# Rotary positions by row swaps inside SBUF in place of a permutation product

## Chip, cores and metric

The kernel runs on one core of a Trainium2 chip. The metric is the time of one launch on the device, in microseconds. All data are fp32 in HBM; the weights are read once per launch.

## What is computed

One inference step of a two-layer backbone on 128 context tokens and 128 latent tokens, side by side as 256 columns. Each layer is a SwiGLU feed-forward half step, a token mixer with three branches, and another feed-forward half step. The mixer has a state-space scan, a differential attention and a pooling branch. Only the attention matters here: its queries and keys of the latent tokens carry two-dimensional rotary positions before the scores. Cut from the reference (`n_freq` is 16, a head has 64 features, `half` is 32):

```python
def rotate(u, pos):
    ang = pos.astype(jnp.float32)[:, None] * inv_freq
    cos = jnp.cos(ang)[None, :, None, None, :].astype(u.dtype)
    sin = jnp.sin(ang)[None, :, None, None, :].astype(u.dtype)
    u1, u2 = u[..., :n_freq], u[..., n_freq:]
    return jnp.concatenate([u1 * cos - u2 * sin, u1 * sin + u2 * cos], axis=-1)

half = DIFF_HEAD_DIM // 2
return jnp.concatenate([rotate(t[..., :half], pos_row), rotate(t[..., half:], pos_col)], axis=-1)

# latent path of the mixer
q = axial_rope(q, rows)
k = axial_rope(k, rows)
k_all = jnp.concatenate([k_ctx, k], axis=1)
s = jnp.einsum('bqhcd,bkhcd->bhcqk', q_blk, k).astype(jnp.float32) * (d ** -0.5)
```

So feature f of a group of 32 has its partner 16 features away: out = t * cos + partner(t) * (plus or minus sin). Scores are sums over the 64 features of a half head, so the order of features inside it is free as long as q, k and the cached keys share it. The keys of the context are an output as well (`new_cache_k`).

## The kernel before

Activations lie feature by token: 128 features on the partitions, 256 tokens on the free axis (0 to 127 context, 128 to 255 latent). Weights come as 486 tiles of 128 x 1024 fp32 (512 KB) in one list, `plan()`. Each is loaded from HBM by SyncE into a `raw` tile (4 buffers), rounded by ScalarE into the high half `wh` (`emit_hi`), and VectorE makes the low half `wl` as raw minus `wh` (`emit_lo`). TensorE then takes three products per 128 x 128 piece (`mm3`, `nat`): wh with the high half of the activations, wh with their low half, wl with their high half. At the end of each tile's products `end()` runs the casts up to 5 tiles and the subtractions up to 4 tiles ahead of the tile in use. The tile `raw` comes free when the subtraction has read it, and the next load waits for that.

The order of instructions is written out at build time. `Pace` is a small cost model: it keeps a clock per engine, a time at which each piece of each tile is ready, and a latency per engine (2.2 us for a DMA). Side work is written as generators (`att_rope`, `att_scores`, `ssd`, `ada_rows` and others). A generator yields the engine that leads its next step and the tiles that the step needs; `advance()`, called after every second weight piece, lets a step go when the model says that its tiles are ready (`due()`; two generators of the list `gens` are looked at together, each up to 4 us ahead of PE's clock). On the chip each engine works through its own queue in that order and waits on semaphores that the framework sets.

In the mixer, the tiles of interest come in the order K (8 tiles, line 1129), V (8 tiles by `nat`, line 1142), z (8 tiles, line 1150), a gate, a branch, a gate, a branch. After the K tiles, `att_scores` and `att_rope` are added as generators (lines 1137 and 1138), and `vc` is loaded (line 1140). `att_rope` (line 1239) makes four rotations per layer, one after another, for the latent columns of q and of k, four heads at a time (a strided 128 x 512 view `t`): a product with the constant `perm` on TensorE into a PSUM tile of tag `s1` (two buffers, shared by all side work), then on VectorE a multiplication with `sin` into the SBUF tile `sw` (tag `t512`, two buffers), a multiplication of `t` with `cos` in place, and an addition. `att_scores` takes the context's scores first ((0, 0) and (0, 1) in `ATT`); those of the latent tokens wait for the entry in `roped` of their four heads. PSUM tiles of the projections have tag `pm` (three buffers). The row sums of the modulation (`ada_rows`) run on VectorE between all this.

Of the kernel before, what the change touches and what calls it, by code (L numbers as in the profile page):

```python
# [13 lines left out]
ALU = mybir.AluOpType  # L14
AX = mybir.AxisListType.X

P = 128
# [18 lines left out]
OFF_Q = 2592  # L36
OFF_K = 3616
OFF_V = 4640
# [57 lines left out]
CST = {}  # L96
_o = 0
for _n, _w in (("ident", 128), ("ones", 128), ("sel", 2), ("uf", 128), ("ub", 128), ("p0", 128), ("p1", 128), ("p2", 128),
               ("p3", 128), ("cos", 128), ("sin", 128), ("perm", 128), ("bm", 16), ("ind", 2)):
    CST[_n] = (_o, _o + _w)  # L100
    _o += _w
CST_W = _o
# [3 lines left out]
def constants():  # L106
    c = np.zeros((P, CST_W), np.float32)
    k = np.arange(P)[:, None]
    m = np.arange(P)[None, :]

    def put(name, a):
        c[:, CST[name][0]:CST[name][1]] = a

    put("ident", k == m)
    put("ones", 1.0)
    put("sel", k % 32 == m[:, :2])
    put("uf", k <= m)
    put("ub", k >= m)
    put("bm", np.where(k < 64, 1.0, -1.0) * (k % 16 == m[:, :16]))
    put("ind", k // 16 % 2 == m[:, :2])  # L120
    for g, w in enumerate(WINDOWS):
        lo = np.clip(m - w // 2, 0, P)
        hi = np.clip(m + w - w // 2, 0, P)
        cnt = (hi - lo).astype(np.float32)
        put(f"p{g}", ((k >= lo) & (k < hi)).astype(np.float32) / cnt - (k == m).astype(np.float32))
    inv = (THETA ** (-np.arange(16, dtype=np.float64) / 16)).astype(np.float32)
    perm = np.zeros((P, P), np.float32)
    for r in range(P):
        d = r % 64
        half, f = d // 32, d % 16  # L130
        pos = (np.arange(P) // GRID_W) if half == 0 else (np.arange(P) % GRID_W)
        ang = pos.astype(np.float32) * inv[f]
        c[r, CST["cos"][0]:CST["cos"][1]] = np.cos(ang.astype(np.float64))
        c[r, CST["sin"][0]:CST["sin"][1]] = np.sin(ang.astype(np.float64))
        if d % 32 < 16:
            perm[r + 16, r] = -1.0
        else:
            perm[r - 16, r] = 1.0
    put("perm", perm)
    return c  # L140


def head_order():
    return [4 * (2 * hf + half) + j for hf in range(2) for j in range(4) for half in range(2)]


def chan_order():
    return np.concatenate([np.arange(h * 64, h * 64 + 64) for h in head_order()])
# [84 lines left out]
def pack_weights(I, seq):  # L233
    out = np.zeros((len(seq), P, 1024), np.float32)
    co = chan_order()
    ho = head_order()
    xcols = np.concatenate([co, np.arange(1024, 1536)]) + OFF_XBC
    zcols = co + OFF_Z
    dcols = np.array([OFF_DT + d * 16 + h for d in range(2) for h in ho])

    def cols(w):
        return w.reshape(KD, P, P).transpose(1, 0, 2).reshape(P, 1024)

    fout = {}
    for i, s in enumerate(seq):
        t, l = s[0], s[1]
        if t == "fin":
            out[i] = cols(I["ffn_w_in"][l, s[2], :, s[3] * P:(s[3] + 1) * P])
        elif t == "fout":
            key = (l, s[2])  # L250
            if key not in fout:
                w = I["ffn_w_out"][l, s[2]].reshape(KF, P, KD, P)
                fout[key] = w.transpose(2, 0, 1, 3).reshape(KD * KF, P, P)
            out[i] = fout[key][s[3] * 8:(s[3] + 1) * 8].transpose(1, 0, 2).reshape(P, 1024)
        elif t == "xbc":
            out[i] = cols(I["w_in"][l][:, xcols[s[2] * P:(s[2] + 1) * P]])
        elif t == "dt":
            w = np.zeros((D, P), np.float32)
            w[:, :32] = I["w_in"][l][:, dcols]
            out[i] = cols(w)  # L260
        elif t == "win":
            out[i] = cols(I["w_in"][l][:, s[2]:s[2] + P])
        elif t == "z":
            out[i] = cols(I["w_in"][l][:, zcols[s[2] * P:(s[2] + 1) * P]])
        elif t == "nat":
            w = I["w_in"][l][s[3] * 2 * P:(s[3] + 1) * 2 * P, s[2]:s[2] + 512]
            out[i] = w.reshape(2, P, 512).transpose(1, 0, 2).reshape(P, 1024)
        elif t == "pool":
            w = I["pool_map"][l].reshape(4, 2, P, 2, P).transpose(0, 3, 1, 2, 4).reshape(16, P, P)
            out[i] = w[s[2] * 8:(s[2] + 1) * 8].transpose(1, 0, 2).reshape(P, 1024)  # L270
        elif t == "br":
            w = I["w_branch"][l, s[2]]
            if s[2] == 0:
                w = w[co]
            out[i] = cols(w[:, s[3] * P:(s[3] + 1) * P])
        elif t == "wout":
            out[i] = cols(I["w_out"][l][:, s[2] * P:(s[2] + 1) * P])
    return out
# [31 lines left out]
def pack_small(I):  # L310
    x = np.concatenate([I["x_prompt"][0], I["x_sample"][0]], 0)
    xT = np.ascontiguousarray(x.T.reshape(KD, P, NT).transpose(1, 0, 2))
    cc = np.stack([I["c_ctx"], I["c"][0]], 0)
    cT = np.ascontiguousarray(cc.T.reshape(KD, P, 2).transpose(1, 0, 2))
    ck = np.ascontiguousarray(I["cache_k"][0].transpose(0, 3, 2, 1))
    cv = np.ascontiguousarray(I["cache_v"][0].reshape(DEPTH, P, 1024))
    ho = head_order()
    st = I["state_ssm"][0]
    h0 = np.zeros((DEPTH, P, 2, 2, 4, 64), np.float32)
    for T in range(8):  # L320
        for half in range(2):
            h = ho[2 * T + half]
            h0[:, 64 * half:64 * half + 64, T // 4, :, T % 4] = st[:, :, h].transpose(0, 3, 1, 2)
    return xT, cT, ck, cv, h0.reshape(DEPTH, P, 1024)
# [99 lines left out]
def backbone(ctx: ExitStack, tc: tile.TileContext, seq, wst, wada, wa0, wrow, xT_d, cT_d, cB_d, ck_d, cv_d, h0_d, prm_d, cst_d,  # L424
             y_d, nk_d, nv_d, ns_d):
    nc = tc.nc
    pace = Pace()
    clk = pace.clk
    V, S, T_, G = (Paced(pace, n, e) for n, e in
                   (("dve", nc.vector), ("act", nc.scalar), ("pe", nc.tensor), ("pool", nc.gpsimd)))  # L430
# [10 lines left out]
    def v3(t, a):  # L441
        return t.rearrange("p (a b) -> p a b", a=a)

    def nm(s):
        uid[0] += 1
        return f"{s}{uid[0]}"
# [10 lines left out]
    def tmp(tag, shape, dt=F32, bufs=None):  # L457
        return tp.tile(shape, dt, tag=tag, name=nm(tag), **({"bufs": bufs} if bufs else {}))
# [12 lines left out]
    def grab(tag, t):  # L471
        free[tag].remove(min(free[tag], key=lambda n: pace.last.get(n, 0.0)))
        return t

    def drop(tag, t):
        free[tag].append(t.tensor.name)

    def ps1(n=512):
        return grab("s1", pp.tile([P, n], F32, tag="s1", bufs=2, name=nm("s1")))
# [16 lines left out]
    def C(name):  # L496
        return cst[:, CST[name][0]:CST[name][1]]
# [66 lines left out]
    def load(out, src):  # L564
        nc.sync.dma_start(out=out, in_=src)
        pace.op("dma", out.free_size() * P * 4 / 360e3, [out], [])

    def load_more(limit):
        while st["load"] < min(limit, st["cap"]):
            i = st["load"]  # L570
            raws[i] = pace.slot("raw", RAW_BUFS, wp.tile([P, 1024], F32, tag="raw", bufs=RAW_BUFS, name=nm("raw")))
            load(raws[i], wst[i])
            st["load"] += 1
# [88 lines left out]
    def ada_load(item):  # L662
        l, i, k = item
        raw = big()
        load(raw, wada[l, k, :, i])
        return raw
# [25 lines left out]
    def ada_rows(us, last):  # L692
        us = list(us)
        s = []
        for b in range(2):
            s.append(big())
            load(s[b], cB_d[:, b])
# [351 lines left out]
    def mixer(l):  # L1049
# [86 lines left out]
        oh, ol = [None, None], [None, None]  # L1136
        add(att_scores(l, q8, kl8, kc3, roped, ats))
        add(att_rope(q, kl, roped))
        vc = big()
        load(vc, cv_d[l])  # L1140
# [98 lines left out]
    def att_rope(q, kl, roped):  # L1239
        for i in range(2):  # L1240
            for t in (v3(q[i], 4)[:, :, P:], v3(kl[i], 4)[:, :, P:]):
                yield "pe", t, "s1"
                ps = ps1(512)
                T_.matmul(ps, lhsT=C("perm"), rhs=t, start=True, stop=True)
                yield "dve", ps
                sw = tmp("t512", [P, 512])
                V.tensor_tensor(out=v3(sw, 4), in0=v3(ps, 4), in1=C("sin").unsqueeze(1).to_broadcast([P, 4, P]), op=ALU.mult)
                drop("s1", ps)
                V.tensor_tensor(out=t, in0=t, in1=C("cos").unsqueeze(1).to_broadcast([P, 4, P]), op=ALU.mult)
                yield "dve", t, sw  # L1250
                V.tensor_tensor(out=t, in0=t, in1=v3(sw, 4), op=ALU.add)
            roped[i] = True
# [563 lines left out]
```

## Time and profile before

| | us |
|---|---|
| median of 3 runs | 1560.96 (1560.48 to 1561.48) |
| the profiled execution | 1561.46 |
| its span, first to last instruction | 1559.70 |
| TensorE busy in it | 1529.8 |
| VectorE busy in it | 1320.7 |
| ScalarE busy in it | 853.8 |

The profile is one execution. Engines are PE (TensorE's matmuls), PEld (its weight loads), DVE (VectorE), ACT (ScalarE), POOL (GpSimd) and SP (SyncE, which issues the DMAs). A matmul's record reaches past the time at which the next one can begin, so the cost of one matmul in a row of them is read from start to start. Rows name a tile written, an arrow, and the tiles read, without buffer numbers; nearly all instructions have line 393 or 565, the helpers that record them, so they are told apart by tile. In the rows below, `s<-big,cst` with 512 columns is the product with `perm`, `t<-s,cst` is the multiplication with `sin`, `big<-big,cst` that with `cos`, and `big<-big,t` the addition. The first four rotations run at 427 to 442 us, the second four at 1179 to 1193 us.

### The profile page before, as it was taken

The page shows a single profiled execution, that of the slowest core. Times are in us where ns is not written, and L with a number is a line of the kernel's source. Part 1 is how long each engine was busy: PE and PEld are TensorE (multiplying, and loading weights), DVE is VectorE, ACT ScalarE, POOL GpSimd, SP SyncE. Part 2 cuts the span into 40 slices and gives each one's busy share as a digit, 9 for nine tenths or more (in the row PEclk, how much of TensorE's full clock was granted, in tenths as well). Part 3 has the DMA queues.
Part 4 walks back from the last instruction along what each step waited for, and adds up shares of the span by engine and source line. Part 5 has one row for each costly group of instructions (what it writes and reads, how often), then busy time and mean ns, then how long its engine had stood idle before and what let it go on. Part 6 is the DMA issues. An engine that isn't in the chain of part 4 may idle for free.

```text
span 1559.7 us, 30787 instructions
## 1 busy us (share of the span) xinstructions
PE 1529.8 (98%) x12062; PEld 1435.4 (92%) x12062; DVE 1320.7 (85%) x2412; ACT 853.8 (55%) x1538; POOL 59.0 (4%) x65
## 2 busy tenths in 40 slices
PE   6999999999999999999999999999999999999997
PEld 4988889999989999999899998998998999999986
DVE  5787698987888998999989999898879899888754
ACT  3564447654667446644447444575555754565442
POOL 0000002000001000100001000100000010010000
PEclk9999999999999999999999999999999999999998
DMA  9688775553664666688765877555466457568652
GB/s 371 215 331 297 264 266 165 186 188 123 237 221 159 230 227 231 217 313 286 254 224 190 297 272 268 178 189 175 143 221 232 162 198 262 175 203 281 217 179 82
DMA packets 98738, 348.26 MB, mean 223 GB/s; under 512 B 10913, under 2 KB 14625, under 8 KB 98465
## 3 DMA queue, kind: packets, MB, share of 16 engines
q1 hardware_dynamic: 98592, 346.30, 64.0%
q8 instruction: 95, 1.56, 0.4%
q14 instruction: 51, 0.41, 0.1%
HBM read 342.06 MB, written 4.19 MB: 222 GB/s over the span
## 4 chain that ended last, share of the span: by engine, by line
PE 78%; issue 12%; DVE 6%; DMA 2%; ACT 1%; POOL 1%; DVEq 0%; POOLq 0%; SPq 0%
PE pm L393 70%; PE s L393 6%; DVE big L393 2%; DVE wl L393 2%; PE pa L393 2%; DVE t1k L393 1%; DMA big<-wada 1%; POOL osr L393 1%; ACT big L393 1%; ACT wh L393 0%; DVE wide L393 0%; DMA x<-xT 0%; DVE sqa L393 0%; ACT L393 0%; DVE x L393 0%
## 5 line engine op out<-in xcount | busy, mean ns | idle before, releaser
L393 PE MATMUL pm<-big,wh 128*128 128x256 f32 (+2 forms) x6568 | 1293.3, 294 | 3.7 <-DVE big L393 2.2
L393 PEld LDWEIGHTS pm<-big,wh 128*128 128x128 f32 x6568 | 1030.0, 189 | 52.7 <-issue 19.7
L393 PE MATMUL pm<-big,wl 128*128 128x256 f32 (+1 forms) x3592 | 1005.1, 281 | 0.0
L393 PEld LDWEIGHTS pm<-big,wl 128*128 128x128 f32 x3592 | 676.8, 188 | 2.2
L393 DVE TENSOR_TENSOR wl<-raw,wh 128x1024 fp32r<-128x1024 f32 x481 | 587.5, 1227 | 9.5 <-ACT wh L393 8.9
L393 ACT CAST wh<-raw 128x1024 fp32r<-128x1024 f32 x481 | 502.0, 1049 | 138.5 <-PE pm L393 101.6
L393 DVE SCALAR_TENSOR_TENSOR big<-big,big 128x1024 f32<-128x1024 f32 x198 | 242.0, 1222 | 12.9 <-DMA big<-wrow 11.6
L393 ACT CAST big<-t1k 128x256 fp32r<-128x256 f32 x88 | 36.0, 409 | 156.5 <-DVE t1k L393 156.5
L393 ACT ACTIVATE big<-x,amod 128x128 fp32r<-128x128 f32 x96 | 33.6, 398 | 101.5 <-DVE x L393 82.6
L393 PE MATMUL pm<-wh,big 128*128 128x512 f32 x256 | 88.5, 409 | 0.0
L393 DVE TENSOR_TENSOR wide<-pm,rb 128x258 f32<-128x258 f32 (+1 forms) x108 | 45.2, 423 | 37.4 <-PE pm L393 30.8
L393 DVE SCALAR_TENSOR_TENSOR x<-pm,mods,x 128x128 f32<-128x128 f32 x152 | 43.7, 346 | 34.3 <-PE pm L393 34.1
L393 ACT COPY big<-pm 128x256 f32<-128x256 f32 (+2 forms) x88 | 31.2, 374 | 74.6 <-PE pm L393 73.8
L393 PEld LDWEIGHTS pm<-wh,big 128*128 128x128 f32 x256 | 48.1, 188 | 13.0 <-issue 2.1
L393 DVE TENSOR_TENSOR big<-t1k,big 128x256 fp32r<-128x256 f32 x128 | 55.8, 440 | 1.6 <-ACT big L393 0.9
L393 ACT ACTIVATE t1k<-wide 128x128 f32<-128x128 f32 (+1 forms) x96 | 33.6, 398 | 38.5 <-DVE wide L393 38.4
L393 PE MATMUL s<-big,big 128*64 128x128 f32 (+5 forms) x544 | 53.3, 303 | 0.0
L393 PE MATMUL pm<-wl,big 128*128 128x512 f32 x128 | 50.3, 393 | 0.0
L393 PEld LDWEIGHTS s<-big,big 128*64 128x64 f32 (+2 forms) x544 | 42.3, 164 | 5.3 <-issue 2.8
L393 ACT ACTIVATE t1k<-pm 128x256 f32<-128x256 f32 x58 | 22.3, 385 | 43.1 <-PE pm L393 43.1
L393 DVE TENSOR_TENSOR big<-big,big 128x256 f32<-128x256 f32 (+1 forms) x64 | 39.9, 623 | 3.3 <-ACT big L393 1.9
L393 DVE SCALAR_TENSOR_TENSOR big<-big,cw,big 128x252 f32<-128x252 f32 (+1 forms) x96 | 39.4, 487 | 2.8 <-ACT big L393 2.7
(146 smaller groups left out, 940.2 us busy)
## 6 DMA issues: line engine op xcount, KB each, us to landing
raw<-wst SPq DMA_DIRECT2D x486, 512.0 KB, 3.7
big<-wrow SPq DMA_DIRECT2D x96, 512.0 KB, 5.0
big<-wada SPq DMA_DIRECT2D x32, 512.0 KB, 5.6
big<-wa SPq DMA_DIRECT2D x16, 512.0 KB, 10.1
big<-cB SPq DMA_DIRECT2D x12, 512.0 KB, 7.7
x<-xT SPq DMA_DIRECT2D x1, 1024.0 KB, 4.9
big<-h SPq DMA_DIRECT2D x2, 512.0 KB, 4.4
ns<-t SPq DMA_DIRECT2D x8, 128.0 KB, 4.9
```

The lines of the kernel that those rows point to most:

```text
L393: r = fn(*a, **k)
```

## The change

The features of q, k and the cached keys are laid out in another order, made on the host in the weights' columns and in the cache: inside each 64 features the partner of a row stands 32 rows away. The constant `perm` goes. In `att_rope` the swapped copy of `t` is made by four transfers from SBUF to SBUF, each of 32 rows x 4 heads x 128 columns (64 KB, in runs of 512 bytes), issued by ScalarE on its own DMA queue (`swap`). The sign is in the constant `sin`. The step that leads a rotation is now one of `act` without a PSUM tile, and the `sin` multiplication reads `sw` in place. In the model each transfer takes 0.3 us on the DMA clock. The written keys `nk` go out in the new order, and the host sorts them back. Number and size of all other instructions stay as they are.

```diff
-               ("p3", 128), ("cos", 128), ("sin", 128), ("perm", 128), ("bm", 16), ("ind", 2)):
+               ("p3", 128), ("cos", 128), ("sin", 128), ("bm", 16), ("ind", 2)):
...
+def pair_order():
+    r = np.arange(P)
+    return r // 64 * 64 + r // 16 % 2 * 32 + r // 32 % 2 * 16 + r % 16
...
-            out[i] = cols(I["w_in"][l][:, s[2]:s[2] + P])
+            w = I["w_in"][l][:, s[2]:s[2] + P]
+            out[i] = cols(w[:, pair_order()] if OFF_Q <= s[2] < OFF_V else w)
...
-    ck = np.ascontiguousarray(I["cache_k"][0].transpose(0, 3, 2, 1))
+    ck = np.ascontiguousarray(I["cache_k"][0].transpose(0, 3, 2, 1)[:, pair_order()])
...
+    def swap(out, src):
+        nc.scalar.dma_start(out=out, in_=src)
+        pace.op("dma", 0.3, [out], [src])
...
             for t in (v3(q[i], 4)[:, :, P:], v3(kl[i], 4)[:, :, P:]):
-                yield "pe", t, "s1"
-                ps = ps1(512)
-                T_.matmul(ps, lhsT=C("perm"), rhs=t, start=True, stop=True)
-                yield "dve", ps
+                yield "act", t
                 sw = tmp("t512", [P, 512])
-                V.tensor_tensor(out=v3(sw, 4), in0=v3(ps, 4), in1=C("sin").unsqueeze(1).to_broadcast([P, 4, P]), op=ALU.mult)
-                drop("s1", ps)
+                for p in range(0, P, 32):
+                    swap(v3(sw, 4)[p:p + 32], t[p ^ 32:(p ^ 32) + 32])
+                yield "dve", sw
+                V.tensor_tensor(out=v3(sw, 4), in0=v3(sw, 4), in1=C("sin").unsqueeze(1).to_broadcast([P, 4, P]), op=ALU.mult)
                 V.tensor_tensor(out=t, in0=t, in1=C("cos").unsqueeze(1).to_broadcast([P, 4, P]), op=ALU.mult)
                 yield "dve", t, sw
                 V.tensor_tensor(out=t, in0=t, in1=v3(sw, 4), op=ALU.add)
...
-    nk = np.asarray(r["nk"]).transpose(0, 3, 2, 1)[None]
+    nk = np.asarray(r["nk"])[:, np.argsort(pair_order())].transpose(0, 3, 2, 1)[None]
```

## Rows read from the trace of the kernel before

**Rows 1.** The page, part 1: busy us, share of the span, instructions.

```profile
PE 1529.8 (98%) x12062; PEld 1435.4 (92%) x12062; DVE 1320.7 (85%) x2412; ACT 853.8 (55%) x1538; POOL 59.0 (4%) x65
```

**Rows 2.** The page, part 4: the chain that ended last, by engine.

```profile
PE 78%; issue 12%; DVE 6%; DMA 2%; ACT 1%; POOL 1%; DVEq 0%; POOLq 0%; SPq 0%
```

**Rows 3.** Windows: stretch; length; busy of PE, PEld, DVE, ACT, POOL; clock; DMA.

```profile
425.00:430.00 5.00, 5.00 (x37) 3.77 (x36) 5.00 (x6) 1.38 (x3) 0.00 (x0) 1.00 0.86 302
430.00:435.00 5.00, 5.00 (x20) 3.43 (x19) 5.00 (x10) 4.11 (x18) 0.00 (x0) 1.00 0.88 288
435.00:440.00 5.00, 5.00 (x24) 3.49 (x24) 5.00 (x8) 2.74 (x4) 0.00 (x0) 1.00 0.63 211
...
450.00:455.00 5.00, 5.00 (x25) 3.61 (x24) 4.18 (x8) 1.62 (x2) 0.00 (x0) 1.00 0.86 288
455.00:460.00 5.00, 5.00 (x39) 4.66 (x37) 2.98 (x9) 4.46 (x13) 0.00 (x0) 1.00 0.79 205
...
470.00:480.00 10.00, 10.00 (x86) 9.49 (x84) 9.82 (x23) 7.58 (x19) 0.00 (x0) 1.00 0.31 108
```

**Rows 4.** PE: all products with `perm` (min/median/max ns); timeline (start us, us) around one.

```profile
L393 PE MATMUL s<-big,cst x16: 590/592/697, 427.8 to 1187.3; 128*128 128x512 f32 x16
...
428.99 0.39 PE L393 MATMUL pm<-wl,big 128*128 128x512 f32 x1
...
429.68 0.39 PE L393 MATMUL pm<-wl,big 128*128 128x512 f32 x1
...
435.33 1.02 PE L393 MATMUL s<-big,cst 128*128 128x512 f32 x2
435.79 0.80 PE L393 MATMUL pm<-wh,big 128*128 128x512 f32 x1
436.42 0.40 PE L393 MATMUL pm<-wl,big 128*128 128x512 f32 x1
```

**Rows 5.** Groups of DVE instructions: busy us, mean ns, idle before.

```profile
L393 DVE TENSOR_TENSOR t<-s,cst 128x512 f32<-128x512 f32 x8 | 5.5, 688 | 0.0
L393 DVE TENSOR_TENSOR big<-big,cst 128x512 f32<-128x512 f32 x8 | 5.5, 688 | 0.0
```

**Rows 6.** Windows of `wl` on DVE; of `wh` on ACT; ACT timeline; ACT groups, 453 to 479.

```profile
0.00:425.90 425.90, 144.16 (x119) 1.00 0.68 240
0.00:443.20 443.20, 149.27 (x123) 1.00 0.68 241
0.00:478.90 478.90, 161.43 (x133) 1.00 0.67 236
...
0.00:425.90 425.90, 124.95 (x120) 1.00 0.68 240
...
426.11 0.43 ACT L393 COPY big<-pm 128x128 f32<-128x128 f32 x2 [1.44 <-PE pm L393]
...
L393 ACT ACTIVATE t1k<-pm 128x256 f32<-128x256 f32 x6 | 2.3, 391 | 4.2 <-PE pm L393 4.2
```

**Rows 7.** Page part 6 (KB, median us to landing); issues of `ns`, of `ck` (ns).

```profile
ns<-t SPq DMA_DIRECT2D x8, 128.0 KB, 4.9
...
nk<-big SPq DMA_DIRECT2D x2, 512.0 KB, 7.1
...
cT<-cT SPq DMA_DIRECT2D x1, 8.0 KB, 1.8
...
L1172 SPq DMA_DIRECT2D ns<-t x8: 423/424/1105, 342.6 to 1141.1; - x8
...
L565 SPq DMA_DIRECT2D big<-ck x2: 384/440/497, 402.4 to 402.8; - x2
...
DMA to landing us min/median/max: 4.9/5.6/6.3
```

**Rows 8.** PE timeline: the scores of latent queries, first and second four heads.

```profile
450.58 1.14 PE L393 MATMUL s<-big,big 64*128 64x256 f32 x8
...
468.08 1.13 PE L393 MATMUL s<-big,big 64*128 64x256 f32 x8
```

More of the change, by code (lines that the diff above doesn't have):

```diff
@@ L126, in constants @@
     inv = (THETA ** (-np.arange(16, dtype=np.float64) / 16)).astype(np.float32)
-    perm = np.zeros((P, P), np.float32)
     for r in range(P):
-        d = r % 64
+        d = pair_order()[r] % 64
         half, f = d // 32, d % 16
         pos = (np.arange(P) // GRID_W) if half == 0 else (np.arange(P) % GRID_W)
[L132 to L139, printed above, removed]
-    return c
+        ang = (pos.astype(np.float32) * inv[f]).astype(np.float64)
+        c[r, CST["cos"][0]:CST["cos"][1]] = np.cos(ang)
+        c[r, CST["sin"][0]:CST["sin"][1]] = np.sin(ang) if d % 32 >= 16 else -np.sin(ang)
+    return c
+def pair_order():
+    r = np.arange(P)
+    return r // 64 * 64 + r // 16 % 2 * 32 + r // 32 % 2 * 16 + r % 16
 def head_order():
```

## The prediction

> **What bounds the kernel now.** First the busy times of the engines [rows 1]: PE works 98% of the span, DVE 85%. Then the chain of work that ended last [rows 2]: PE holds 78% of it, so the end is mostly a sum of PE work. An average over the span doesn't say what the rotation costs, so next the stretch where it runs in layer 0, in windows [rows 3]. The reader is to see three things there. PE is busy 5.00 of every 5.00 us, at the full clock, 2.4 GHz. DVE is busy 5.00 of 5.00 as well from 425 to 440, has holes at 450 to 460 (4.18 and 2.98 of 5.00), and is nearly full again at 470 to 480. ACT has 1.38, 4.11 and 2.74 of 5.00. So what leaves PE here shortens the program, as long as DVE, which makes the low half of every weight tile, isn't made later than its lead allows. The lead is read from counts [rows 6], below.
>
> **What the change takes away.** Per layer four products with `perm`, eight in all; each is two records of one fp32 matmul, so sixteen [rows 4]. The duration of a record (590 ns) overlaps its neighbours, so I take start to start. The matmuls of the V projection stand 0.23 us apart: three of them from 428.99 to 429.68. The single product begins at 435.33, and the second matmul after it at 436.42; without 0.23 for the first one, the product holds PE for 436.42 - 0.23 - 435.33 = 0.86 us. Eight of these are 8 x 0.86 = 6.9 us of a PE that has no idle time beside them. The first product of a layer shows about 0.1 more, just behind the scores; I leave that out, since the scores hand over to the next product anyway. The two PSUM tiles of tag `s1` are also held less; nothing waits for them in this stretch, so that is worth nothing.
>
> **What it adds on DVE.** The multiplication with `sin` reads the swapped copy from SBUF instead of PSUM. Nearest rows [rows 5]: from PSUM 688 ns, and the multiplication with `cos`, of the same size and all in SBUF, 688 ns. Difference nothing. What is new is its wait: it now needs four transfers to have landed, and on DVE's queue stand behind it the subtractions `wl`, on which PE lives, the row sums of the modulation, and the softmax steps.
>
> **What it adds on ACT.** 16 issues per layer on ACT's queue, 32 in all. The trace has no DMA issued by ACT. The nearest rows are SP's [rows 7]: 0.42 us for `ns`, 0.38 at best and 0.50 for `ck`, so from 16 x 0.38 to 16 x 0.50, or 6.1 to 8.0 us per layer; below that, almost nothing, if ACT's engine works on what is queued while its sequencer issues. I take 0.42, that is 1.7 us per group of four and 6.7 us per layer. Behind these issues ACT holds the casts `wh`, the copies out of PSUM and the exponentials. ACT had (5.00 - 1.38) + (5.00 - 4.11) + (5.00 - 2.74) = 6.8 us free in the first three windows of [rows 3], and at 425.90 it had made 120 casts where DVE had made 119 subtractions [rows 6]: its casts are as far ahead of PE. A late copy out of PSUM is met by a third `pm` tile. So: nothing on PE; were that cover gone, up to 1.7 us a group, 13.6 us in all.
>
> **When the swapped copy lands.** Each transfer is 64 KB in runs of 512 bytes. Bounds from [rows 7]: 1.8 us for 8 KB, 7.1 for the 512 KB of `nk`, one of which goes out in this very stretch; `ns`, 128 KB, takes 4.9. I take about 4, a little below `ns`, since that writes to memory and the swap doesn't. With three issues before the last one that is 3 x 0.42 + 4 = 5.3 us from the first issue to the landing of all four. The planner gives the DVE step free only when its model says so: 4 x 0.3 + 2.2 = 3.4 us, counted from its DMA clock, on which the loads in front stand too (512 KB are 1.46 us there; `vc` is loaded just before the first rotation). So it hands the step to DVE after 3.4 to about 6 us, and meanwhile gives DVE other work. Real less planned: between 1.26 + 1.8 - 6 = -3 (no wait at all) and 1.26 + 7.1 - 3.4 = +5. I take 1 us of DVE standing still per rotation, four per layer.
>
> Here a rule speaks against the change. In the trace two `ck` loads issued 0.4 us apart, each in 512-byte runs, landed 4.9 and 6.3 us after issue [rows 7]: their latencies lie on top of each other. The Trainium skill, "DMA: Bandwidth & Descriptors", section "Rules for kernel authors", says to coalesce many small transfers, since under 64 KB one pays mostly overhead; and by the fixed 2.0 us of its section "Anatomy of one DMA" four transfers one after another would be over 8 us (an estimate from that page). By that each rotation would leave DVE about 2 to 5 us short; by the row it isn't so, because the four are in flight together.
>
> **What covers those 4 us.** The lead of the low halves [rows 6]. At 425.90 PE begins the first V tile, number 122 of the list (the copy of the last K tile follows at 426.11); DVE has begun 119 + 5 = 124 low halves, the five being those of the start. So two finished tiles lie ahead of the one in work, with the third in making, about 8 us at 2.8 us a tile (12 products of 0.23). At 443.20 it is the same: 128 begun, and PE, after four V tiles, at the 126th. At 478.90 it is thinner: 138 begun, the 138th just done, while PE works on the seventh z tile, the 136th (six z tiles have been copied out by 479); some 5 us. DVE makes up for lost time in the holes of 450 to 460, before that point. A PE that is 3.5 us earlier per layer takes as much from the lead: 5 - 3.5 = 1.5 us are left. So the cover holds in the sum, but not by much; I book 0.5 us for all places together where it doesn't.
>
> **The chain of rotations gets longer** and that is covered. A rotation took about 3 us of the chain (products at 427.8, twice at 430.8, at 435.3), and now takes 6 to 7, so the second ends near 440 and the fourth near 455. Their readers, the scores over latent keys, begin at 450.58 for the first four heads and at 468.08 for the others [rows 8].
>
> **Sum.** Profiled execution: 1561.46 (span 1559.70 and 1.76 around it). Less 6.9, plus 0.5: 1555.1. That execution stands 0.5 above the median of the runs, so 1560.96 - 6.4 = **1554.6 us**. A second queue in use might lengthen the start or the end; the trace shows only that all around the span is 1.76 us, so that is 0 to 1.8, and I take 0.
>
> **The rivals.**
> 1. DVE waits for the transfers and PE for DVE: slower. The mechanism is DVE's first-in-first-out queue at the `sin` multiplication. The four waits of a layer fall within some 25 us; cover is the 8 us of lead and 2.8 us of holes between 450 and 460, so from 2.7 us a rotation on PE begins to lose, and from 2.7 + 3.45 / 4 = 3.6 us it loses all that it won. At the upper bound of 5 us PE loses 20 - 10.8 = 9.2 us per layer, and the time is 1561 - 6.9 + 18.4 = 1572.5; at 4.5 it is 1568.5. For it: DVE full from 425 to 440, and `nk`, `cv` and weight loads in flight there. Against: the planner already waits, and fills the wait.
> 2. DVE is the real bound of the stretch, and PE's gain comes back as waits for low halves between 460 and 520: about 1561, between 1558 and 1564. For it: DVE at 9.82 of 10 at 470 to 480, and a lead of 5 us there. Against: 2 of 5 us free just before.
> 3. ACT's issues hold back copies out of PSUM: with two of eight groups badly placed, 2 x 1.7 = 3.4 us come back, 1558. Against: the third `pm` tile, and ACT's free time.
> 4. It doesn't take the product's time away, because PE would have stood still there: 1561. Against it are 5.00 of 5.00 us; no chance of its own.
> 5. PE gains more than the products, from the `s1` tiles or the 0.1 behind the scores: 1551 to 1552.
>
> **How the numbers follow.** My forecast (1552.5 to 1557) 0.56; rival 1, 0.12; rival 2, 0.18; rival 3, 0.11; rival 5, 0.03. About 0.2%, 3.1 us, is what a measurement of this kernel can tell from no change. Faster by more than that, below 1557.8: 0.56 + 0.03 + 0.09 of rival 3 = 0.68. Within it: 0.18 + 0.02 = 0.20. Slower, above 1564.1: 0.12. The range for 8 in 10 takes in the forecast, rival 3 and most of rival 2: 1552.0 to 1563.0.
>
> **What would show it.** The records with `cst` of 512 columns gone from PE and PE still busy 5.00 of 5.00 in the same windows: step right. DVE idle before `t<-t,cst`, released by a DMA, over 2.7 us each and then PE idle for `wl`: rival 1. PE idle for `wl` with no such wait: rival 2. ACT issues at 0.4 us and PE idle for `pm`: rival 3. Landings of the swaps at 3 to 5 us; at 7 my term for them is wrong. If the planner's new order moves a stall elsewhere, by more than 2 us, the sum is wrong for a reason that no step of it holds.

## The result, and the profile after

| | us |
|---|---|
| before, median of 4 runs beside it | 1561.22 (1560.48 to 1562.17) |
| changed, median of 4 runs | 1572.39 (1570.56 to 1575.12) |
| ratio, 95% interval | 1.0071 (1.0057 to 1.0084) |
| profiled execution after, its span | 1573.09, 1571.3 |

The change makes the kernel 11.2 us slower; 1554.6 was predicted, and 1563.0 was the upper end. First, PE in part 1 of the page after (busy us, share, instructions), against [rows 1]:

```profile
PE 1527.0 (97%) x12046; PEld 1435.2 (91%) x12046; DVE 1319.9 (84%) x2412; ACT 854.0 (54%) x1540; POOL 60.4 (4%) x65
```

Sixteen matmul records fewer, and PE is busy 2.8 us less, but the span is 11.6 longer: PE now stands still. The waits of PE (us in total, times, longest) name where; the lines shown are those that the kernel before does not have in this size:

```profile
PE pm L393 <- DVE x L393: 10.2, 1, 10.2
...
PE s L393 <- ACT big L393: 3.0, 2, 1.9
...
PE pm L393 <- DVE wide L393: 2.1, 4, 1.4
...
PE pm L393 <- ACT big L393: 1.0, 1, 1.0
```

The large one is a single hole, and it isn't at the rotations. It stands at the output projection of layer 1, some 140 us behind the last of them. Windows of the changed kernel (columns as in [rows 3]), and then its timeline there, first SP, then ACT, DVE and PE (start us, us, engine, line, operation, and in brackets the wait before it):

```profile
1330.00:1340.00 10.00, 10.00 (x87) 10.00 (x86) 7.52 (x14) 4.61 (x6) 0.00 (x0) 1.00 0.52 169
1340.00:1350.00 10.00, 2.49 (x21) 2.28 (x20) 3.90 (x7) 2.11 (x2) 0.00 (x0) 0.72 0.57 198
1350.00:1360.00 10.00, 7.04 (x38) 6.78 (x39) 9.25 (x23) 5.98 (x13) 0.00 (x0) 0.60 0.45 136
```

```profile
1337.37 0.90 SPq L565 DMA_DIRECT2D big<-cB  x2
1338.31 0.95 SPq L565 DMA_DIRECT2D big<-wrow  x2
...
1343.35 1.06 ACT L393 ACTIVATE big<-big 128x1024 f32<-128x1024 f32 x1 [5.77 <-DMA big<-cB]
...
1345.93 1.23 DVE L393 SCALAR_TENSOR_TENSOR big<-big,big 128x1024 f32<-128x1024 f32 x1 [7.87 <-DMA big<-wrow]
...
1351.93 0.60 DVE L393 SCALAR_TENSOR_TENSOR x<-pm,mods,x 128x128 f32<-128x128 f32 x2
...
1352.68 0.77 PE L393 MATMUL pm<-big,wh 128*128 128x256 f32 x2 [10.20 <-DVE x L393]
```

Read upward: PE waits for an addition to `x`; that waits for `mods`; `mods` waits for four multiplications of two row sums on DVE (1.22 us each, `big<-big,big` of 128x1024); these wait for two loads of `wrow`; and in front of them ACT has waited for two loads of `cB`. Loads of `cB` belong to a batch of row sums: page part 6 has 12 of them before and 14 after (KB, median us to landing). The code explains the extra batch:

```profile
big<-cB SPq DMA_DIRECT2D x12, 512.0 KB, 7.7
big<-cB SPq DMA_DIRECT2D x14, 512.0 KB, 7.3
```

```
if not row_todo or st["cur"] >= last - HOLD:      # in ada_rows: batch ends, HOLD = 5 tiles before `last`
    us.clear()
...
def need(*ms):                                    # called by gated_add at the first output tile
    late = [i for i, it in enumerate(row_todo) if it[:2] in ms]
    if late:
        side["slow"].append(Side(ada_rows([0] * (late[-1] + 1), 1 << 30)))
    settle(lambda: all(m in ada_done for m in ms))
```

The output projection of layer 1 needs 88 row sums, two instructions each. A batch gets its places from DVE's free time in the model and ends five tiles before its stage. Counted in the trace up to the first addition to `x` in that projection, DVE has run 182 such instructions before (88 row sums and 6 others) and 178 after: two row sums are missing, and `need` makes them there, with everything standing still. The two counts (us in total, mean ns, idle time before), before and after:

```profile
L393 DVE SCALAR_TENSOR_TENSOR big<-big,big 128x1024 f32<-128x1024 f32 x182 | 222.4, 1222 | 11.2 <-DMA big<-wrow 10.0 <-ACT big L393 0.4
L393 DVE SCALAR_TENSOR_TENSOR big<-big,big 128x1024 f32<-128x1024 f32 x178 | 216.8, 1218 | 12.2 <-DMA big<-wrow 10.2 <-ACT big L393 1.2
```

Up to 480 us, behind the rotations of layer 0, SP has issued 19 loads of `wrow` before and 18 after; up to 620 us it is 29 and 28, and up to 800 us 51 and 49. So the changed kernel falls one behind at the rotations and two behind by 800 us. (The runs e1 and e2 below are one behind at 480 us too, and have caught up by 620.)

In the hole PE's clock falls: PE stands still from 1342.5, and the granted clock is 0.50, that is 1.2 GHz, from 1346 to 1357 and 1.00, 2.4 GHz, from 1359 on (the windows above, 0.72 and 0.60, hold both levels). Groups of three products that start 0.36 us apart at 1358.4 start 0.64 apart at 1357.3. Together: the first product with the low half of the tile `wout` 2 of layer 1 starts 2.4 us earlier than before (1339.7 against 1342.1), that of `wout` 4 10.8 later (1358.6 against 1347.8), so the hole costs 13.2 us, of which 10.2 + 0.3 are standing still and most of the rest the lower clock.

What the change itself added looks as follows. Instructions by tile (ns min/median/max, first and last start), page part 6 (KB, us to landing), and the range of the landings:

```profile
L569 ACTq DMA_DIRECT2D t<-big x32: 592/612/1523, 427.2 to 1199.6; - x32
L393 DVE TENSOR_TENSOR t<-t,cst x8: 679/681/687, 438.8 to 1205.3; 128x512 f32<-128x512 f32 x8
...
DMA to landing us min/median/max: 2.0/4.5/7.2
```

```profile
t<-big ACTq DMA_DIRECT2D x32, 64.0 KB, 4.4
```

In the view of the tiles `t`, none of what DVE sat idle for is a DMA. The 3.0 us of `PE s <- ACT big` are the second scores of each layer, which must wait until ACT has read the first ones (here the first layer):

```profile
427.67 1.16 PE L393 MATMUL s<-big,big 64*128 64x128 f32 x16
436.48 1.16 PE L393 MATMUL s<-big,big 64*128 64x128 f32 x16 [1.16 <-ACT big L393]
```

They stand 8.8 us behind the first; before it was 13.1, with no wait:

```profile
426.70 1.16 PE L393 MATMUL s<-big,big 64*128 64x128 f32 x16
...
439.77 1.16 PE L393 MATMUL s<-big,big 64*128 64x128 f32 x16
```

In layer 1 the wait is 1.86. The 1.0 us of `PE pm <- ACT big` follows there: a product of the V projection needs a `pm` tile that ACT is to copy out, and the copy stands in ACT's queue behind the second exponentials, which begin at 1189.67:

```profile
1192.43 1.11 ACT L393 COPY big<-pm 128x512 f32<-128x512 f32 x2
1193.10 0.50 PE L393 MATMUL pm<-wh,big 128*128 128x512 f32 x1 [0.98 <-ACT big L393]
```

The line `DVE wide`, 1.4 us at the longest, stands at the second FFN of layer 1; the experiments come back to it.

### The profile page after: what moved, and what is told of

The parts are those of the page before. It is cut to its first block, busy times and chain, and to the rows that moved or that the text cites. A ratio compares the mean times of both kernels' runs of the same rounds, so it can differ in the third digit from the quotient of the medians.

```text
span 1571.3 us, 30803 instructions
## 1 busy us (share of the span) xinstructions
PE 1527.0 (97%) x12046; PEld 1435.2 (91%) x12046; DVE 1319.9 (84%) x2412; ACT 854.0 (54%) x1540; POOL 60.4 (4%) x65
## 4 chain that ended last, share of the span: by engine, by line
PE 76%; issue 12%; DVE 7%; DMA 3%; ACT 2%; POOL 0%; SPq 0%; DVEq 0%; POOLq 0%; ACTq 0%
PE pm L393 68%; PE s L393 6%; DVE big L393 2%; DVE wl L393 2%; PE pa L393 2%; DVE t1k L393 1%; DMA big<-wrow 1%; ACT big L393 1%; ACT wh L393 1%; DMA big<-cB 0%; DVE wide L393 0%; DMA big<-wada 0%; DMA x<-xT 0%; DMA raw<-wst 0%; DVE sqa L393 0%
## 5 line engine op out<-in xcount | busy, mean ns | idle before, releaser
L393 PE MATMUL pm<-big,wh 128*128 128x256 f32 (+2 forms) x6568 | 1295.8, 294 | 14.8 <-DVE x L393 10.2
L393 POOL TENSOR_TENSOR rsr<-rsv,halfc 128x2 f32<-128x2 f32 x9 | 6.3, 698 | 923.3 <-DVE rsv L393 923.3
```

Of the source, the lines that this page charges most:

```text
L393: r = fn(*a, **k)
```

## Experiments

All times are medians; each run has its own runs of the kernel before beside it (1561.3 to 1561.6), and the ratio to those decides. A profile is one execution, and executions differ by 1 to 2 us in their first 50 us alone, so only waits and local distances are compared between profiles. In the expectations, "row sum" at the first addition to `x` counts single instructions: two of them are one row.

| run | kernel | us | ratio (95%) |
|---|---|---|---|
| e1_hold4 | changed, HOLD 4 | 1559.44 | 0.9987 (0.9977 to 0.9998) |
| e2_noswap | changed, no exchange at all | 1557.54 | 0.9974 (0.9965 to 0.9984) |
| e3_before_late_rows | before, two row sums left over | 1574.64 | 1.0088 (1.0074 to 1.0101) |
| e4_act_cost | changed, ACT's issues in the model | 1560.64 | 0.9995 (0.9986 to 1.0004) |
| e5_rows_sooner | changed, ROW_LAG 1.0 | 1565.61 | 1.0025 (1.0016 to 1.0034) |
| e6_noswap_rows_sooner | no exchange, ROW_LAG 1.0 | 1555.71 | 0.9969 (0.9958 to 0.9980) |
| e7_before_rows_sooner | before, ROW_LAG 1.0 | 1560.68 | 1.0006 (0.9996 to 1.0016) |
| e8_sync_queue | e5 with transfers on SP's queue | 1566.00 | 1.0028 (1.0017 to 1.0040) |
| e9_cast_gate | e1 and a limit on casts | 1556.73 | 0.9969 (0.9957 to 0.9982) |
| e10_rows_sooner_cast_gate | e5 and the limit | 1559.90 | 0.9988 (0.9979 to 0.9998) |
| e11_cast_gate_exps_first | e9 and the limit at V | 1560.06 | 0.9986 (0.9978 to 0.9995) |
| **e12_table_load_told** | e9 and the table load in the model | **1553.95** | **0.9952 (0.9934 to 0.9970)** |
| e13_before_same_mends | before, with e12's three edits | 1560.76 | 1.0004 (0.9995 to 1.0013) |
| e14_noswap_same_mends | e12 with no exchange | 1555.33 | 0.9965 (0.9953 to 0.9977) |

### Is it the left-over row sums?

```diff
-HOLD = 5
+HOLD = 4
```


> The changed kernel with HOLD = 4 in place of 5, so that the row sums of a mixer may be begun one weight tile later; the plan then has all 16 row sums in the mixer of layer 0 and none left over at the first output tile of layer 1. Theory A (the loss is the two left-over row sums, made while PE stands still: the first use of output tile 4 of layer 1 lies 13.2 us later against before than that of output tile 2): 1572.4 - 13.2 = 1559, 1557 to 1561. Theory B (the loss is DVE's wait for the transfers, as in rival 1 of the prediction): HOLD does not touch that, 1571 to 1573.

```diff
-CAP = {..., ("mix", 1): (16,), ...}
+CAP = {..., ("mix", 1): (14,), ...}
```
(in the kernel before)


> The kernel before, products and all, with the number of row sums allowed in the mixer of layer 1 cut from 16 to 14, so that two are left over and made at the first output tile, as in the changed kernel. Theory A: 1561.2 + 13.2 = 1574, 1572 to 1576. Theory B: the two left-over sums are hidden or cheap, 1561 to 1564.

HOLD 4 gives the missing rows their places, the trace has 12 loads of `cB`, 182 instructions up to the first addition, and no hole: 1559.44, 13 us less than the changed kernel. The other way round, the kernel before with two row sums left over and nothing else becomes 13.2 us slower, with the same hole; its waits of PE:

```profile
PE pm L393 <- DVE x L393: 10.0, 1, 10.0
```

One cause added and taken away, 13 us each time: this is shown. In the kernel before, HOLD 4 changes no instruction, so it isn't a gain of its own.

### What of the products' 6.9 us comes out?

```diff
                 sw = tmp("t512", [P, 512])
-                for p in range(0, P, 32):
-                    swap(v3(sw, 4)[p:p + 32], t[p ^ 32:(p ^ 32) + 32])
-                yield "dve", sw
-                V.tensor_tensor(out=v3(sw, 4), in0=v3(sw, 4), in1=C("sin")...)
+                yield "dve", t
+                V.tensor_tensor(out=v3(sw, 4), in0=t, in1=C("sin")...)
```


> The changed kernel without any transfer: the multiplication with sin reads t itself, so the exchange of partners is left out; neither products nor transfers are there, HOLD is 5 and the plan has no left-over row sums. Both A and B: the products' PE time comes out in full, 1561.2 - 6.9 = 1554.3, 1553 to 1556. Rival 2 of the prediction (DVE is the bound, PE's gain comes back as waits): 1558 to 1562.

```diff
     def swap(out, src):
         nc.scalar.dma_start(out=out, in_=src)
+        pace.op("act", 0.45, [], [])
         pace.op("dma", 0.3, [out], [src])
```


> The changed kernel where the planner also books 0.45 us of ACT's time for each of the 32 issues; the plan then has no left-over row sums either. Theory A: at least the 13.2 us are gone, 1559 or less. If the two waits of PE for ACT at the second scores (1.2 us in layer 0, 1.9 and 1.0 in layer 1) come from issues that the planner did not know of, they go as well: 1555 to 1557. If they come from something else: 1558 to 1560. Theory B: 1571 to 1573.

Without product and transfers only 4 us come out, where 5 to 8 were expected. So something besides the transfers takes back PE's gain even here. Telling the model of ACT's issues moved the row sums enough to save the left-over ones too, but gained nothing beyond HOLD 4. At 1560.64 it lies above all that was forecast for it but theory B: the waits at the second scores are still 2.4 us in all, so they don't come from issues that the planner did not know of, and `pm <- DVE wide` (2.0) and `pm <- ACT big` (1.3) are there too.

The trace of e2_noswap and e1_hold4 shows a wait of 2.3 and 2.1 us in PE, `pm <- DVE wide`, at the start of the second FFN of layer 1, where the kernel before has at most 0.5 under that name (in all, times, longest; before, then e1):

```profile
PE pm L393 <- DVE wide L393: 1.3, 5, 0.5
PE pm L393 <- DVE wide L393: 3.1, 4, 2.1
```

Two reasons were open: late row sums straight before the first addition to `x`, which use up the lead of the low halves (theory C), or a DVE that is full anyhow (theory D).

```diff
-ROW_LAG = 0.7
+ROW_LAG = 1.0
```


> The changed kernel with ROW_LAG 1.0 in place of 0.7, so that the planner gives the row sums a higher claim on DVE; nothing is computed otherwise. All 88 row sums of the output projection are made in time, as with HOLD 4 (1559.4), but here the last of them lies three weight tiles ahead of the first addition to x in layer 1, and not straight before it (with HOLD 4 one row sum of 2 x 1.22 us, or half of one, stands there). Theory C (the gain of 6.9 on TensorE is partly eaten at the first output tiles and at the start of the second FFN of layer 1, because late row sums have used up the lead of the low halves on DVE): 1556.5 to 1558, 1.5 to 3 us below HOLD 4, with PE's wait at the start of that FFN about 1.5 us shorter. Theory D (DVE as a whole is nearly full, wherever its row sums stand): the same as HOLD 4, 1558.5 to 1560.5. The first theory, A (the left-over row sums alone made the change slower), only asks that it stays under 1561.

> As the run without the exchange of partners (neither product nor transfers, DVE multiplies the features themselves with the sine: the exchange is left out), with ROW_LAG 1.0. Without ROW_LAG it took 1557.5, so that of the 6.9 us of matmuls only 4 came out; there two row sums stood straight before the first addition to x in layer 1, here none. Theory C: 1554.5 to 1556, so that 5.5 to 6.5 of the 6.9 come out. Theory D: 1557 to 1558.5, no more than before. Against the kernel with transfers and the same ROW_LAG it gives the price of the transfers themselves: about 2 us by the difference of the two runs with the old ROW_LAG (1559.4 - 1557.5).

> The kernel before with ROW_LAG 1.0: the control for the two above. Theory C: the kernel before has 5.5 to 7 us of lead of the low halves at the end of the mixer and its last row sum already stands four tiles ahead of the first addition to x, so that nothing is to be had: 1560.5 to 1562, within 0.1% of it. Theory D's rival reading, that a higher claim of the row sums helps any order: 1558 to 1560.

Neither theory holds as it stands. Without the exchange the wait goes and 1555.71 was measured (by the median 1.8 less, by the ratio 0.8, within the intervals); the control didn't move. But the changed kernel became 6 us slower than with HOLD 4, although the lead of the low halves is back (at the tile `wout` 3 of layer 1 it is 3.4 us from the end of the subtraction to its use, as before; 1.8 with HOLD 4). The wait at the FFN is now 4.0:

```profile
PE pm L393 <- DVE wide L393: 5.4, 6, 4.0
```

Here is ACT's queue there, of e5_rows_sooner, of e1_hold4 and of the kernel before:

```profile
1364.71 1.05 ACT L393 CAST wh<-raw 128x1024 fp32r<-128x1024 f32 x1 [2.19 <-DMA raw<-wst]
1370.00 1.04 ACT L393 CAST wh<-raw 128x1024 fp32r<-128x1024 f32 x1 [4.24 <-DMA raw<-wst]
1370.95 0.37 ACT L393 COPY rb<-s 128x256 f32<-128x256 f32 x1
```

```profile
1365.24 1.04 ACT L393 CAST wh<-raw 128x1024 fp32r<-128x1024 f32 x1 [1.53 <-DMA raw<-wst]
1366.20 0.36 ACT L393 COPY rb<-s 128x256 f32<-128x256 f32 x1
```

```profile
1365.59 1.05 ACT L393 CAST wh<-raw 128x1024 fp32r<-128x1024 f32 x1 [2.24 <-DMA raw<-wst]
1367.95 0.37 ACT L393 COPY rb<-s 128x256 f32<-128x256 f32 x1 [1.31 <-PE s L393]
```

`rb` is the reciprocal of the norm; every eviction of that FFN's first tiles (`wide<-pm,rb`) needs it. Before, its copy waits for PE's sums. In the changed kernel and its two variants the planner has put one cast more ahead of it (428 casts of high halves, not 427); in e5_rows_sooner that cast waits 4.24 us for its weight load, in e1_hold4 1.53. ACT works in order, so the copy, DVE's eviction and PE wait with it.

### A cast in front of the norm (theory G)

```diff
-                end(later, SWAP_I)
+                end(later, SWAP_I, 1 if (l, f) == (1, 1) and box["rb"] is None else 0)
```


> The changed kernel with HOLD 4, and besides in layer 1's second FFN no weight tile is prepared a tile further ahead while the reciprocal of the norm (rb) isn't there yet (less=1 in end): so ACT copies rb after 426 casts of high halves instead of 428 (before: 427). Theory G (the wait of 2.1 us at that FFN with HOLD 4, 4.0 with ROW_LAG 1.0, is there because in ACT's queue a cast that waits for its weight load stands ahead of the copy of rb): PE's wait at this place falls to about 0.5 us, 1.5 us less in all: 1557.5 to 1558.5 against 1559.4 with HOLD 4. Rival H (the loads themselves are late because the lead of the low halves on DVE has been used up; the cast only stands in their way by chance): the wait reappears one tile later as a wait for the high or the low half, and the time stays at 1559 to 1560.

> The changed kernel with ROW_LAG 1.0 (1565.6) and the same limit on casts in the second FFN of layer 1. Theory G: the wait of 4.0 us before the second weight tile of that FFN goes to about 0.5, and with it 3.5 us: 1561.5 to 1562.5; what is left over 1559.4 then lies elsewhere (some 1.4 us at layer 0's output projection by the trace). If theories C and G are both right it would come down to 1557 to 1559, since the lead of the low halves at the first output tiles of layer 1 is 3.4 us here and 1.8 with HOLD 4. Rival H: 1564 to 1566.

With HOLD 4 the limit brings 1556.73, 2.7 us less and below the forecast of theory G; with ROW_LAG 1.0 it brings 5.7 us, 1559.9. The second lies between what G alone and what C and G together forecast. The longest wait `pm <- DVE wide` is down to 0.5 and 0.2 us, and ACT's copy waits for PE's sums again, here e9_cast_gate:

```profile
1361.01 0.37 ACT L393 COPY rb<-s 128x256 f32<-128x256 f32 x1 [3.17 <-PE s L393]
```

The 2.7 us are no larger than the intervals of the two runs; the 5.7 are clear of them. Theory G is confirmed and H refuted; what ROW_LAG 1.0 still costs beside e9 (3 us) lies elsewhere and was not followed up.

### The second scores

Is it ACT's queue, loaded with issues?

```diff
     def swap(out, src):
-        nc.scalar.dma_start(out=out, in_=src)
+        nc.sync.dma_start(out=out, in_=src)
```


> The changed kernel with ROW_LAG 1.0 and its 32 transfers issued on the SP queue, not on ACT's; the planner's order of everything else is the same. The transfers' price is some 2 us, and the trace has it as two waits of PE for ACT at the second pair of scores (1.2 + 1.2). Theory E (ACT is held up by issuing them, 0.61 us each, and by an issue that waits for its source): these waits shrink, 1 to 2 us below the kernel with ROW_LAG 1.0 on ACT's queue, unless SP's weight loads, which then stand behind a transfer that waits for its source, come late. Theory F (the waits come from the planner's order, in which the second scores stand nearer to the first and the exps between them take their time on ACT whoever issues the transfers): the same time within 1 us.

The waits of PE there are 2.4 us in all with either queue, and the time is the same (1566.0 and 1565.6): theory F. The Trainium skill, "DMA: Bandwidth & Descriptors", section "Issuing engines are not separate DMA queues", says that another issuing engine saves only its sequencer's time; the run agrees. On SP's queue these issues take 0.60 us in the median (0.59 to 1.60), as on ACT's.

Or the cast that waits 2.7 us ahead of the exponentials?

```diff
         (end of nat's tile)
-            end()
+            end(less=1)
```


> As the first of these (HOLD 4, the limit in the FFN), and besides the same limit in the projections of V (less=1 in nat), so that the exponentials of the first scores stand ahead of a high cast which waits 2.7 us for PE in ACT's queue, as in the kernel before (126 casts before the first exponential, with HOLD 4 127). Theory G, applied to the second scores: the two waits of PE for ACT there (1.2 + 1.2 us) go or fall below 0.3 each, 2 us less than the first of these runs: 1555.5 to 1557. Against it: preparing tiles one later costs PE a wait for the high half when a V projection's tiles are used (3 to 5 us of lead there), and two row sums again stand straight before the first addition to x in layer 1, about 1 us at the FFN; then 1557.5 to 1559. The reverse, that the exponentials' place in the queue has nothing to do with it: the waits stay at 1.2 us each.

The cast now stands behind the exponentials, and the wait stays (1.05 us in layer 0): ACT's table load begins at 431.56, as soon as DVE has the scaled maximum (431.31 to 431.5), so the cast did not hold it. Refuted. The kernel became 3.3 us slower than e9 and, at 1560.06, slower than any forecast for it; where, beyond this place, was not settled. What is left is the chain maximum, table load, eight exponentials, which the model has shorter than it is:

```diff
                 yield "act", mx
+                if it == 0:
+                    pace.op("act", 1.28, [], [])
```


> As the run with HOLD 4 and the limit on casts in the FFN (1556.7), and besides the planner is told, ahead of the first exponentials of each layer, that ACT needs 1.28 us for its table there (one planner entry, no instruction more). Theory I (the two waits of PE at the second scores stand there because the planner has ACT's exponentials end earlier than they do: maximum, table load 1.28 and eight exponentials 2.75 us on the way; not because of the transfers): the second scores move three matmuls later in PE's queue, some 0.6 us, in layer 0 and as many in layer 1, and the waits fall from 1.2 to about 0.5 us each: 1555 to 1556.5. If the waits stay at 1.2, or the scores' place has nothing to do with it: 1556.5 to 1557.5.

The table load of 1.28 us (the Trainium skill, "ScalarE: Activation LUTs", section "What ACT_TABLE_LOAD costs", has about 1283 ns and behind it a drain of about 1380; the trace agrees on the load, but shows only 1.31 us in all from the end of the instruction before it to the start of the next activation) has no entry in the model. With one, PE has three matmuls more to do ahead of these scores, both waits fall to less than a half, and the run is the fastest, 1553.95, a little below the forecast of theory I:

```profile
430.22 1.28 ACT L393 ACT_TABLE_LOAD   x1
...
434.47 1.16 PE L393 MATMUL s<-big,big 64*128 64x128 f32 x16 [0.44 <-ACT big L393]
...
1182.40 1.16 PE L393 MATMUL s<-big,big 64*128 64x128 f32 x16 [0.51 <-ACT big L393]
```

(The table load of layer 0, and PE's second scores of the two layers.) The gain on e9, 2.8 us, is no larger than the intervals of the two runs. These waits account for 1.4 of it. The wait of 1.0 us for ACT's copy of `pm` in layer 1, which e9 has and e12 hasn't, accounts for 1.0 more: the copy (1186.57) now stands ahead of the second exponentials. The rest was not separated.

### Are the mends worth as much in the kernel before?

> The kernel before with the three mends of the fastest version (HOLD 4, the limit on casts in the second FFN of layer 1, the table load told to the planner). Theory J (the 7.5 us are the change's own: the mends only undo what its new order broke; the kernel before has none of the three faults, with no row sum left over, rb copied after 427 casts, no wait at the second scores): 1560 to 1562, within 0.1% of the kernel before. Theory K (the mends help any order): 1555 to 1558, and then the change itself is worth only 1 to 4 us.

> The same three mends with neither product nor transfers (the exchange of partners is left out). Against the run with transfers (1553.95) it gives the price of the 32 transfers when the order has no holes. Theory J: the transfers are covered, and 1553 to 1554.5 comes out. If they still cost PE what its two waits at the second scores show (0.4 + 0.5 us) or more: 1552 to 1553. Two row sums stand straight before the first addition to x in layer 1 here, which may cost up to 1 us at the FFN.

The kernel before doesn't move with the same three edits (1.0004): these mends are worth something only where the change's order broke something. They were chosen in the traces of the changed kernel, though; whether other hints would speed up the kernel before was not tried, apart from ROW_LAG 1.0. And the transfers cost nothing that can be measured in the time: with no exchange at all 1555.33 (0.9953 to 0.9977), slower than forecast, with transfers 1553.95 (0.9934 to 0.9970). The two waits at the second scores that e12 keeps (0.44 and 0.51 us) are absent without the exchange.

## Why the prediction was wrong, step by step

- **PE, -6.9.** Right in size. With the order mended the changed kernel is 0.48% (0.30 to 0.66) below the kernel before, 7.5 us (4.7 to 10.3); the sum had -6.4. It also shows in place: between the same two low-half products around each layer's rotations (425.79 to 580.05 and 1169.11 to 1300.09 us in the kernel before) PE needs 3.9 and 3.9 us less in e12, and 3.5 and 3.4 in e14, without the exchange; 2 x 3.45 was said. The changed kernel itself has 3.2 in layer 0 and only 0.4 in layer 1, where its waits for ACT of 1.86 and 0.98 us stand. The forecast of 1554.6 was met only by a kernel whose planner was given three hints more.
- **DVE's multiplication.** Right: 681 ns against 688 of [rows 5].
- **ACT's issues.** Mis-sized, and no wait of PE is traced to them: 0.61 us each, not 0.42, so 2.4 us a group. What stands ahead of them in ACT's order goes on beside them (at 443.69 to 446.27 four issues run beside exponentials and a cast without a gap); what stands behind waits for them (four issues end at 1197.42, and the cast behind them begins at 1197.53, after 2.41 us idle). So the lower bound that the prediction named, almost nothing, holds only in part. PE has no wait for ACT there, and moving the issues to SP did not change the time.
- **Landing.** Right for one transfer: about 4 was taken, 4.4 is the median of page part 6, 2.0 to 7.2 in all. Too short for the group: 5.3 was said from the first issue to the landing of all four, and the eight groups took 4.3 to 8.2, about 6.5 in the middle. So the four overlap, as the `ck` rows of [rows 7] had it: four groups were done in 4.3 to 6.0 us, and landing one after another, over 8 us, is not what the trace shows, though one group took 8.2. What the Trainium skill says of small transfers ("DMA: Bandwidth & Descriptors", "Rules for kernel authors") agrees with the trace itself: 64 KB took 4.4 us, and the 512 KB of a weight tile 3.9.
- **DVE standing still, 1 us a rotation.** Too much: no such wait in the changed kernel, one of 1.1 us in layer 0 of e12. The planner gave the step late enough and filled the time.
- **Longer chain of rotations.** Longer than said: the second addition ended at 446, the fourth at 463 (440 and 455 were said). The scores over latent keys still found it done: 447.97 and 467.61, no wait, against 450.58 and 468.08 of [rows 8].
- **The cover, +0.5 for all places.** This step failed. It asked only whether the low halves stay ahead, and they did: PE has no wait of weight for `wl` in the stretch. But it took the order of everything else as given. The change alters the model's clocks (a DMA of 3.4 us in place of a product, DVE free earlier), so the planner places other work anew: two row sums missed a deadline, one cast went ahead of `rb`, the second scores moved 4 us closer to the first. In place of 0.5 us, the row sums cost 13.2 us (e3; HOLD 4 gives back 13.0). The other two mends brought 2.7 us (e9) and 2.8 us (e12), where the traces show waits of 2.0 and 2.4 us gone.
- **Around the span.** 1.8 us after, as 1.76 before: right.

Rival 1 gave nearly the measured time (1572.5), but for a reason that isn't there: DVE waited for no transfer. The agreement is luck. Rival 2 did not come true: PE has no wait for low halves between 460 and 520, and what it waits for more than before, outside the hole, are evictions (`wide`), scores and copies of `pm`. Rival 3 had the right mechanism, something queued ahead on ACT, with the wrong thing in front: a cast ahead of `rb`, and in layer 1 exponentials ahead of the copies of `pm`, and not an issue. The last sentence of the prediction, on a stall that the new order moves elsewhere, names what happened; it had no price and no chance in the rivals. It could have had one: the batch's deadline and `need` stand in the code, two left-over row sums are a load (`wrow` lands 5.0 us after its issue in part 6 of the page before) and four instructions of 1.22 us with PE idle, 9.9 us, and the profile of before shows how close it was: 88 row sums were made when 88 were needed.

## What to carry to other kernels

Where a planner writes the order, a change of one step's cost or engine is a change of the whole order: before pricing instructions, look for what has a deadline or a place that is just met (a count that exactly suffices, a copy that stands one cast behind another) and price missing it. When a change that should gain loses, look for a single hole first, and far from the edit; then mend the order, repeat the same mends in the kernel before as a control, and only then judge the idea. In a queue that works in order, a cheap step that everybody waits for must not stand behind one that waits for a load.

## What the runs showed of the hardware

- Issuing one of the 64 KB transfers (32 rows, runs of 512 bytes) took ACT 0.61 us (0.59 to 1.52) and SP 0.60 (0.59 to 1.60, e8), against 0.33 to 0.42 for SP's loads of 512 KB. Of ACT's arithmetic, what stood ahead of the issues went on, and what stood behind waited for them (2.41 us at 1197.53).
- Four transfers of 64 KB from SBUF to SBUF, 0.6 us apart, land 2.0 to 7.2 us after their issue, and all four 4.3 to 8.2 us after the first issue, beside weight loads. They cost the kernel nothing measurable (1553.95 us with them, 1555.33 without).
- After 10 us of standing still PE ran on at a granted clock of 0.50 until 1357, and 0.73 until 1359, at 0.64 in place of 0.36 us for a group of three products: the hole cost more than its length, 13.2 us for 10.5.
